# A hybrid convolution and attention block: eight plain products for four query and key jobs, another order for the scaling of x and for the last pair

## Chip, cores and metric

One core of one Trainium2 chip runs the kernel. The metric is the time of one execution on the device in microseconds (us); the number that stands for the kernel is the median of several executions.

## The reference

The block takes x (1 x 2048 x 1024, float32). After an RMS norm with a shift and a scale that come from a small vector c, one projection with 10,240 columns feeds everything else: a causal convolution of 31 taps with two gate inputs, 12 heads of dilated window attention, and the gates that mix the two branches. Cut to what matters here:

```python
mod = jax.nn.silu(c) @ w_ada + b_ada
shift, scale, gate = jnp.split(mod, 3, axis=-1)
h = rms_norm(x, norm_w) * (1.0 + scale) + shift
z = h @ w_in
a, b, g_conv, q, k, v, g_attn, m_conv, m_attn = jnp.split(z, SPLIT_POINTS, axis=-1)
u = depthwise_causal_conv(a * sigmoid(b), conv_w, conv_b)
y_conv = (silu(layer_norm(u, ...)) * silu(g_conv)) @ w_conv_out
q = rope(rms_norm(q, q_norm_w), positions)
k = rope(rms_norm(k, k_norm_w), positions)
outs, lses = dilated_window_attention(q, k, v, window, dilation)   # three groups of four heads
o = sum(softmax(lses) * outs)
y_attn = (o * silu(g_attn)) @ w_attn_out
y = sigmoid(m_conv) * y_conv + sigmoid(m_attn) * y_attn
x = x + gate * (y @ w_out)
```

## The kernel before

**The projection.** The tokens are worked in two halves of 1024. A job is a block of 256 columns for one half. The block is cut in four (token quarters times column halves), and `qkv_quad` (L530) or `quad` (L346) computes it with seven products in place of eight, in the manner of Strassen and Winograd: `PRODUCTS` (L167) pairs A11, A12, A22 and the sums S1 to S4 of quarters of h with B11, B21, B22 and the sums T1 to T4 of quarters of the weights. One product (`product`, L338) is 12 matmuls of 128x512: both factors are split in a high and a low half, and three of the four terms are taken over four pieces of the contraction.

**The weights.** `column_steps` (L260) loads four blocks of weights by SP's queue (names wB11 and so on), makes T1 to T4 on GpSimd (L274), splits each in a high half (ScalarE, L279) and a low half (L280; GpSimd, or VectorE for the products that `QKV_LO` lists), and in the first half also stores each T to DRAM (L285). The second half loads these T's again, seven loads a job rather than four.

**What follows a product.** In `qkv_quad` the results are gathered in two PSUM banks, z and s: four copies on ScalarE (L546) and three additions on VectorE a job. `rotate` (L615) then normalises and rotates q and k: squares on ScalarE, sums over the head by matmuls (pss), rows, a transpose (L655), a root on GpSimd (L664), for k a transpose back and a spreading matmul (L684, L693), 12 VectorE operations for the rotation, and a store to `qk_d`. `turn_v` (L600) transposes v on TensorE.

**The order of the work.** A slot is one product. `slots` lists which job's which product stands in each slot. All other work hangs in an agenda by slot and place (`at_slot`, L506), and the main loop (L1541) writes it out slot by slot; this written order is the order on TensorE, and on VectorE, ScalarE, GpSimd and SP's queue too, but for a stretch in the gates where the scheduler orders the latter four. Weights are asked for five slots ahead and split three slots ahead (`AHEAD`, L39).

The first half begins with plain V jobs of two pairs (slots 0 to 15, `plain_quads`: products without sums). Slots 16 to 127 hold the jobs of `QUADS` (L1081): q and k of pairs 0 and 1, then q, k and v of pairs 2 to 5. From slot 128 come the gates and the convolution's a and b, and the attention of the first half. The second half starts at slot 282 with V, has its first four q and k jobs at some 296 to 325 and its gates from about 408 to 561. The output projections follow.

**Work without a slot of its own.** The convolution's VectorE operations (`conv_parts`, L388) wait in `conv_todo`. After each slot the main loop adds `PACE` (L42) to a credit, takes off what VectorE operations of the slot cost by the kernel's own estimate (`Counted`, L200), and runs pieces while the credit lasts:

```python
credit = min(max(credit, -2.0) + PACE[i >= half_jobs] - spent[0], 2.0)
while conv_todo and credit > 0.35:
    run_conv(1)
```

The second half's x is loaded, squared (`later_x`, `later_square`, L1320) and scaled (`later_scale`, `later_sum`, L1358, L1365; 32 VectorE operations in four groups) while the first half's q, k and v jobs run. The scalings are laid by hand into slots 42 to 67 by a list `room` (L1392). Only then is the SBUF that they use given to the attention (`free_at`, L1454). At the turn of the halves the quarters A12, A22 and S1 to S4 of the second half land from DRAM and are split (`quarter_split`, L182; names landing).

## Time and profile before

| what | value |
|---|---|
| runs, us | 2378.17, 2378.13, 2377.22; median 2378.13 |
| profiled execution, own time | 2384.58 us |
| its span | 2382.7 us |
| its mean granted TensorE clock | 0.989 |
| GpSimd (POOL) busy in the span | 1120.5 us, 47% |
| HBM traffic | 284.98 MB read, 164.24 MB written |

The span goes from the first to the last instruction of the profiled execution; its own time is 1.9 us more, and lies 6.45 us above the median of the runs. In the profile, PE is TensorE, PEld its weight loads, DVE VectorE, ACT ScalarE, POOL GpSimd and SP the engine that issues the DMAs. The page gives busy time by engine and by group; the windows give it for a stretch (busy time, count of instructions, granted clock, share of the DMA engines, GB/s); the waits give what ended an engine's idle time. A recorded matmul's time overlaps the next one's, and a few per cent of the matmuls may be missing from the records.

### The profile page before, as it was taken

To read this page: it belongs to the slowest core of one execution; us is meant where nothing else is said; L and a number is where in the kernel's file an instruction comes from. 1 tells how busy PE (TensorE), PEld (TensorE's weight loads), DVE (VectorE), ACT (ScalarE), POOL (GpSimd) and SP (SyncE) were. 2 spreads that over 40 slices of the span, in tenths; PEclk is the share of its full clock that TensorE was granted. 3 is DMA by queue.
4 is the path that set the end of the run, shared out by engine and by line. 5 is a ranking of instruction groups with operands and counts; after the bars stand their busy time and mean duration, and the time that the engine had idled before them with its cause. 6 is when DMAs were issued, how large, how long until landed. Compare 5 with 4: busy or idle time off the path is not lost. (4 is left out here: it accounts for less than half of the span.)

```text
span 2382.7 us, 34400 instructions
## 1 busy us (share of the span) xinstructions
PE 2293.4 (96%) x11386; PEld 1864.2 (78%) x11386; DVE 1740.3 (73%) x2838; ACT 1113.5 (47%) x2267; POOL 1120.5 (47%) x878
## 2 busy tenths in 40 slices
PE   6899899999999999989999999999999999999999
PEld 4677678887888887867788887877888888888887
DVE  6768874657979789847757557599997957796644
ACT  4754355555654444644455444554444444332221
POOL 2366544455557788936433333445666740000221
PEclk9999999999999999999999999999999999999999
DMA  7656766676654454643665665756444579875553
GB/s 258 193 174 222 234 175 205 194 219 202 197 171 156 159 189 151 203 150 115 181 191 174 208 186 179 232 153 194 137 137 144 168 250 321 290 236 188 182 161 102
DMA packets 304107, 451.54 MB, mean 190 GB/s; under 512 B 29236, under 2 KB 132788, under 8 KB 303928
## 3 DMA queue, kind: packets, MB, share of 16 engines
q1 hardware_dynamic: 289656, 423.62, 56.2%
q10 hardware_dynamic: 14272, 25.72, 2.9%
q8 instruction: 90, 1.47, 0.3%
q14 instruction: 89, 0.73, 0.1%
HBM read 284.98 MB, written 164.24 MB: 189 GB/s over the span
## 5 line engine op out<-in xcount | busy, mean ns | idle before, releaser
L280 POOL TENSOR_TENSOR slT<-wT,shT 128x512 fp32r<-128x512 f32 x188 | 260.6, 1387 | 312.4 <-ACT shT L279 294.9
L280 POOL TENSOR_TENSOR slB<-wB,shB 128x512 fp32r<-128x512 f32 x164 | 219.1, 1337 | 187.8 <-ACT shB L279 176.7
L279 ACT ACTIVATE shB<-wB 128x512 fp32r<-128x512 f32 x234 | 147.7, 631 | 180.5 <-issue 34.8
L280 POOL TENSOR_TENSOR slT<-wB,shT 128x512 fp32r<-128x512 f32 x98 | 132.7, 1357 | 144.7 <-ACT shT L279 110.8
L208 DVE SCALAR_TENSOR_TENSOR ce<-us,pair_taps,ce 128x512 f32<-128x512 f32 x240 | 180.8, 753 | 5.9
L279 ACT ACTIVATE shT<-wT 128x512 fp32r<-128x512 f32 x192 | 120.7, 628 | 129.1 <-POOL slB L280 23.9
L208 DVE SCALAR_TENSOR_TENSOR ce<-ut,chan,ce 128x512 f32<-128x512 f32 x240 | 180.4, 751 | 0.8
L208 DVE SCALAR_TENSOR_TENSOR cq<-ut,chan,cq 128x512 f32<-128x512 f32 x208 | 156.3, 751 | 4.5 <-ACT cq L409 4.3
L208 DVE CUSTOM_DVE_ANT_0 sm<-ps,mask,rqq 128x256 f32<-128x256 f32 (+1 forms) x192 | 78.1, 444 | 95.1 <-PE ps L837 36.0
L274 POOL TENSOR_TENSOR wB<-wB,wB 128x512 f32<-128x512 f32 x80 | 113.2, 1415 | 54.6 <-DVE slB L208 46.0
L279 ACT ACTIVATE shT<-wB 128x512 fp32r<-128x512 f32 x120 | 75.4, 628 | 71.6 <-PE paab L342 32.6
L137 POOL TENSOR_SCALAR stf<-stf 128x4 f32<-128x4 f32 x4 | 1.9, 474 | 180.2 <-DVE stf L1656 143.5
L893 PE MATMUL po<-v,pT 128*128 128x128 f32 x560 | 81.8, 277 | 2.4 <-ACT pT L870 1.4
L1828 ACT ACTIVATE yh<-yq 128x512 fp32r<-128x512 f32 x48 | 27.4, 624 | 119.8 <-POOL yq L1822 46.2
L893 PEld LDWEIGHTS po<-v,pT 128*128 128x128 f32 x560 | 75.6, 192 | 9.2 <-ACT pT L870 1.9
L208 DVE TENSOR_TENSOR slB<-wB,shB 128x512 fp32r<-128x512 f32 x70 | 55.4, 791 | 30.6 <-ACT shB L279 24.4
L856 ACT ACTIVATE sm<-sm,osb 128x256 f32<-128x256 f32 (+1 forms) x128 | 58.7, 463 | 10.6 <-issue 3.5
L274 POOL TENSOR_TENSOR wT<-wB,wB 128x512 f32<-128x512 f32 x40 | 56.2, 1407 | 2.4
L865 PE MATMUL ptp<-ident,sm 128*128 128x128 f32 x332 | 52.4, 274 | 4.4 <-DVE stm L208 3.9
L865 PEld LDWEIGHTS ptp<-ident,sm 128*128 128x128 f32 x332 | 41.1, 140 | 18.9 <-issue 4.6
L1887 DVE TENSOR_TENSOR xt<-xt,oa 128x512 f32<-128x512 f32 x32 | 22.0, 687 | 45.8 <-PE oa L1900 45.8
L274 POOL TENSOR_TENSOR wB<-wB,wT 128x512 f32<-128x512 f32 x40 | 54.6, 1364 | 0.0
(833 smaller groups left out, 7803.8 us busy)
## 6 DMA issues: line engine op xcount, KB each, us to landing
wB<-in_w_in_dram SPq DMA_DIRECT2D x274, 256.0 KB, 4.0
wT<-tT_d SPq DMA_DIRECT2D x152, 256.0 KB, 3.0
tT_d<-wB SPq DMA_DIRECT2D x114, 256.0 KB, 3.7
qk<-qk_d SPq DMA_DIRECT2D x96, 256.0 KB, 4.0
v_d<-vev SPq DMA_DIRECT2D x48, 256.0 KB, 3.5
qk_d<-spare_hi SPq DMA_DIRECT2D x48, 256.0 KB, 4.0
qk_d<-spare_lo SPq DMA_DIRECT2D x48, 256.0 KB, 4.1
v<-v_d SPq DMA_DIRECT2D x96, 128.0 KB, 3.9
```

What stands on the lines that cost most here:

```text
L137: nc.gpsimd.tensor_scalar(scratch, src, EPS, None, op0=ALU.add)
L208: return f(out, *args, **kw)
L274: nc.gpsimd.tensor_tensor(dst, x0, x1, op=ALU.subtract)
L279: nc.scalar.activation(h, q[name], AF.Copy)
L280: eng.tensor_tensor(l, q[name], h.bitcast(F32), op=ALU.subtract)
L856: nc.scalar.activation(sm[:, a:z], sm[:, a:z], AF.Exp, scale=-1.0, bias=box["low"][i], accum_out=box["total"][i])
L865: nc.tensor.transpose(pt[:, c : c + P], box["sm"][:, c : c + P], ident)
L893: nc.tensor.matmul(po[:, P * i : P * i + P], box["pT"][:, c : c + P], vt, start=(m == 0), stop=(m == count[i] - 1))
L1828: nc.scalar.activation(h, src, AF.Copy)
L1887: add = lambda dst, ps: tc.keep_in_program_order(nc.vector.tensor_tensor(dst, dst, ps, op=ALU.add))
```

## The change

- The first half's (Q,0), (K,0), (Q,1), (K,1) become `qkv_plain` jobs: eight plain products each on A11, A21, A12, A22 with the four loaded weight blocks. No T's, no additions; four copies by ScalarE, the banks z and s in turn; all four low halves on GpSimd. The kernel has 566 products in place of 562, and all slots behind these jobs count four more.
- A21 stays in its buffer until then, so S4, which takes that buffer, is parked in DRAM (`s4_d`, stored in slots 15 to 18, loaded again in 44 to 47).
- The second half's jobs of the same columns find no stored T's, so they make them afresh on GpSimd, with four loads, and split the weights of products 1, 3 and 5 on VectorE.
- The second half's x is loaded and squared a slot apart rather than two, and its 32 scalings are taken from the credit like the convolution's pieces (`run_later`). The attention's memory opens at slot 65 (`LATER_END`).
- `PACE` has a value for each of four stages: 2.75, 3.05, 2.5, 2.85 in place of 2.95.
- The last pair runs k, q, v in place of q, k, v; the stores of its results lose their special places, and the convolution's tiles open a slot earlier.

The diff, cut to its core:

```diff
-PACE, AGAIN = (2.95, 2.95), 12
+PACE, AGAIN = (2.75, 3.05, 2.5, 2.85), 12
+PLAIN_QK, LATER_END = 4, 65
 MANUAL, ORDER_END = (True, True), 6
-LATER_X, LATER_ROOM, LATER_BUSY = 21, 2, 1
+LATER_X = 20
...
+    PLAIN_8 = (("B11", "A11", 0), ("B11", "A21", 1), ("B21", "A12", 0), ("B21", "A22", 1),
+               ("B12", "A11", 2), ("B12", "A21", 3), ("B22", "A12", 2), ("B22", "A22", 3))
+
+    def plain_columns(c0, c1):
+        q, got = {}, []
+        last = []
+        where = {"B11": (0, c0), "B21": (1, c0), "B12": (0, c1), "B22": (1, c1)}
+
+        def fetch(n):
+            name = PLAIN_8[n][0]
+            if n % 2 == 0:
+                t = q[name] = wr.tile([P, 4, P], F32, tag="wr", name=f"w{name}_q{c0}")
+                nc.sync.dma_start(t.rearrange("p k c -> p (k c)"), w_in[where[name][1] // P, where[name][0]])
+
+        def step(n):
+            name = PLAIN_8[n][0]
+            if n % 2 == 0:
+                last[:] = (ws.tile([P, 4, P], F32R, tag=f"s{hl}", name=f"s{hl}{name}_q{c0}") for hl in "hl")
+                nc.scalar.activation(last[0], q[name], AF.Copy)
+                nc.gpsimd.tensor_tensor(last[1], q[name], last[0].bitcast(F32), op=ALU.subtract)
+            got.append(tuple(last))
+
+        return got, step, fetch, None
+
+    def qkv_plain(half, which, pair, got):
+        u0 = 2 * pair
+        g = GROUPS[u0 // NH]
+        reg = [scratch_pair() for _ in range(2)]
+        n = f"{'qkv'[which]}{half}_{pair}"
+        cut, place = token_views(g)
+        rotate(half, which, u0, g, reg, n, slots_of[half, which, pair])
+        ps = {}
+        for m, (_, part, c) in enumerate(PLAIN_8):
+            done = c in ps
+            if not done:
+                ps[c] = bank("zs"[c % 2], f"pp{c}{n}")
+            product(part, ps[c], got.pop(0), not done, done)
+            if done:
+                nc.scalar.activation(place(reg[c // 2], c % 2), cut(ps[c]), AF.Copy)
+            yield
...
-        s0 = at[6] + (u0 == 10)
+        s0 = at[6]
...
-        e4, e5, e6 = at[4], at[5], at[6]
+        e4, e6 = at[4], max(at.values())
...
+            if 7 in at:
+                sq = ((at[3], 0, 0, "act2"), (e4, 1, 0, "act2"), (e6, 0, 1, "act2"), (e6 + 1, 1, 1, "act"))
...
-            start = e6 + 1
+            start = e6 + 1 - (u0 == 10 and which == 0)
...
-            at_slot(e6 + 7, store(0), "vec" if u0 == 10 else "store")
-            at_slot(e6 + 7 + (u0 < 10), store(1), "vec" if u0 == 10 else "load")
+            at_slot(e6 + 7, store(0), "store")
+            at_slot(e6 + 8, store(1), "load")
...
-    QUADS = [(Q, 0), (K, 0), (Q, 1), (K, 1), *((w, p) for p in range(2, 6) for w in (Q, K, V))]
+    QUADS = [(Q, 0), (K, 0), (Q, 1), (K, 1), *((w, p) for p in range(2, 5) for w in (Q, K, V)), (K, 5), (Q, 5), (V, 5)]
...
-        chain = [(qkv_quad, half, *q) for q in QUADS]
+        if half == 0:
+            for q in QUADS[:PLAIN_QK]:
+                slots += [(len(jobs), n) for n in range(8)]
+                jobs.append((qkv_plain, half, *q))
+        chain = [(qkv_quad, half, *q) for q in QUADS[PLAIN_QK if half == 0 else 0 :]]
...
-            return column_steps(half, c0, c0 + P, QKV_LO[half][g])
+            return column_steps(half, c0, c0 + P, QKV_LO[half and (g, cb) not in QUADS[:PLAIN_QK]][g])
...
-        at_slot(17 + k // 2, lambda k=k: part_of("S4", k, hf[4 + k, 0], vec), "act2")
+        at_slot(15 + k, lambda k=k: nc.sync.dma_start(s4_d[k], hf[4 + k, 0]), "store")
+
+    last_a21 = slots_of[0, K, 1][5]
+    parked = {}
+
+    def s4_load(k):
+        parked[k] = wide_raw(f"s4_{k}")
+        nc.sync.dma_start(parked[k], s4_d[k])
+
+    for k in range(4):
+        at_slot(last_a21 - 1 + k, lambda k=k: s4_load(k), "load")
+        at_slot(last_a21 + 1 + k, lambda k=k: quarter_split(0, "S4", k, parked.pop(k), vec), "act2")
...
-            at_slot(LATER_X + 2 * j + 1 + c, lambda j=j, c=c: later_square(j, c), "act2")
-    LATER_0 = LATER_X + 18
+            at_slot(LATER_X + j + 1, lambda j=j, c=c: later_square(j, c), "act2")
+    LATER_0 = LATER_X + 10
...
+    later_todo, later_from = [], {0: LATER_0 + 4, 1: LATER_0 + 4}
+    for k in range(2):
+        at_slot(LATER_0 + 1, lambda k=k: later_load(k), "store")
     for k in range(4):
-        at_slot(LATER_0 + 1 if k < 2 else free[k - 2], lambda k=k: later_load(k), "store")
-        room = [r for r in room if r >= max(when, LATER_0 + 4)]
-        work = [lambda k=k, i=i: later_scale(k, i) for i in range(4)]
+        later_todo += [(k, lambda k=k, i=i: later_scale(k, i)) for i in range(4)]
...
-            work.append(lambda k=k, args=args: later_sum(k, *args))
-        for f in work:
-            when = room.pop(0)
-            at_slot(when, f)
-        free.append(when + 3)
-    later_done = when + 3
+            later_todo.append((k, lambda k=k, args=args: later_sum(k, *args)))
+
+    def run_later(s):
+        k, f = later_todo.pop(0)
+        f()
+        if k < 2 and later_todo[0][0] != k:
+            at_slot(s + 3, lambda: later_load(k + 2), "store")
+            later_from[k + 2] = s + 6
...
-    free_at = [later_done, 0]
+    free_at = [LATER_END, 0]
...
-            k6 = slots_of[half, K, pair][6]
+            q6, k6 = (max(slots_of[half, w, pair].values()) for w in (Q, K))
...
-            ready = max(k6 + 11, v6 + 7, free_at[half])
+            ready = max(q6 + 10, k6 + 11, v6 + 7, free_at[half])
...
-        at_slot(q_end + 7, lambda half=half: conv_open(half), "enter")
+        at_slot(q_end + 6, lambda half=half: conv_open(half), "enter")
...
-        credit = min(max(credit, -2.0) + PACE[i >= half_jobs] - spent[0], 2.0)
+        stage = (i >= gates_start[0]) + (i >= half_jobs) + (i >= gates_start[1])
+        credit = min(max(credit, -2.0) + PACE[stage] - spent[0], 2.0)
         spent[0] = 0.0
-        while conv_todo and credit > 0.35:
-            run_conv(1)
+        while credit > 0.35 and (conv_todo or later_todo and s >= later_from.get(later_todo[0][0], s + 1)):
+            if conv_todo:
+                run_conv(1)
+            else:
+                run_later(s)
```

VectorE, around the first q job of the first half (q0_0), before; slT and slB are low halves of weights, S4_lo the low half of a sum, spare_hi the job's result, to which pbq and pcq are added, and tm its rotation:

```order
L208 TENSOR_TENSOR S3_lo_0_816<-hf3_1_184,S3_hi_0_815 128x512
L208 TENSOR_TENSOR S4_lo_0_955<-hf4_0_177,S4_hi_0_954 128x512
L208 TENSOR_TENSOR S4_lo_0_955<-hf5_0_178,S4_hi_0_954 128x512
L208 TENSOR_TENSOR spare_hi_168<-s1q0_0_937,pbq0_0_960 128x128x4
L208 TENSOR_TENSOR S4_lo_0_955<-hf6_0_179,S4_hi_0_954 128x512
L208 TENSOR_TENSOR S4_lo_0_955<-hf7_0_180,S4_hi_0_954 128x512
L208 TENSOR_TENSOR slB22_0_3584_1017<-wB22_0_3584_752,shB22_0_3584_1016 128x512
L244 CAST pick0_1039<-edge_145 32x128 x2
L208 TENSOR_TENSOR spare_hi_168<-spare_hi_168,pcq0_0_1020 128x128x4
L208 TENSOR_TENSOR slB21_0_5120_1077<-wB21_0_5120_903,shB21_0_5120_1076 128x512
L208 TENSOR_TENSOR spare_hi_168<-spare_hi_168,pcq0_0_1020 128x128x4
```

The same place in the changed kernel:

```order
L210 TENSOR_TENSOR S1_lo_0_777<-hf7_1_189,S1_hi_0_776 128x512
L210 TENSOR_TENSOR hf7_0_181<-hf7_0_181,hf3_0_177 128x512
L210 TENSOR_TENSOR S3_lo_0_810<-hf3_1_185,S3_hi_0_809 128x512
L246 CAST pick0_1001<-edge_146 32x128 x2
L210 SCALAR_TENSOR_TENSOR tmq0_0_00_1122<-spare_hi_169,hw_139,cos0_999 128x512
L210 SCALAR_TENSOR_TENSOR tmq0_0_01_1124<-spare_hi_169,hw_139,sin0_1000 128x512
L210 SCALAR_TENSOR_TENSOR spare_hi_169<-spare_hi_169,hw_139,sin0_1000 128x512
L210 SCALAR_TENSOR_TENSOR spare_hi_169<-spare_hi_169,hw_139,cos0_999 128x512
L210 TENSOR_TENSOR spare_hi_169<-spare_hi_169 128x512
```

The additions of pbq and pcq and the low halves of weights no longer stand there, nor S4's splits; behind S3 come the table rows and the rotation at once.

VectorE at the turn of the halves, before; A22_lo is the last of the landing quarters, cq, co, ce, ca and usum are pieces of the convolution, and pcv is V's bank that is added to its result:

```order
L208 SCALAR_TENSOR_TENSOR A22_lo_1_9842<-landingA22_2_9792,mod_139,A22_hi_1_9841 128x512
L208 TENSOR_TENSOR slT1_1_6912_9872<-wB11_1_6912_9628,shT1_1_6912_9871 128x512
L208 SCALAR_TENSOR_TENSOR cq0_7_9429<-ut0_7_9110,chan_133,cq0_7_9429 128x512 x4
L208 SCALAR_TENSOR_TENSOR co0_7_9910<-ut0_7_9110,chan_133,cq0_7_9429 128x512
L208 TENSOR_TENSOR ca0_7_9912<-ce0_7_9431,co0_7_9910 128x511
L208 COPY ca0_7_9912<-ce0_7_9431 128x1
L208 COPY odd_tail_136<-co0_7_9910 128x1
L208 SCALAR_TENSOR_TENSOR ce0_7_9431<-ce0_7_9431,pair_taps_134,co0_7_9910 128x512
L208 SCALAR_TENSOR_TENSOR ce0_7_9431<-us0_7_9702,pair_taps_134,ce0_7_9431 128x512 x3
L208 TENSOR_TENSOR slB22_1_6656_9939<-wB22_1_6656_9596,shB22_1_6656_9938 128x512
L208 SCALAR_TENSOR_TENSOR ce0_7_9431<-us0_7_9702,pair_taps_134,ce0_7_9431 128x512 x2
L208 TENSOR_TENSOR slB22_1_6912_9958<-wB22_1_6912_9634,shB22_1_6912_9957 128x512
```

And in the changed kernel:

```order
L210 SCALAR_TENSOR_TENSOR A22_lo_1_9813<-landingA22_2_9764,mod_140,A22_hi_1_9812 128x512
L210 TENSOR_TENSOR slT1_1_6912_9842<-wB11_1_6912_9601,shT1_1_6912_9841 128x512
L210 SCALAR_TENSOR_TENSOR ce0_7_9243<-us0_7_9371,pair_taps_135,ce0_7_9243 128x512 x5
L210 SCALAR_TENSOR_TENSOR ca0_7_9559<-us0_7_9371,pair_taps_135,ce0_7_9243 128x512
L210 TENSOR_TENSOR usum0_5250<-usum0_5250,ca0_7_9559 128x1024
L210 TENSOR_TENSOR slB22_1_6656_9904<-wB22_1_6656_9570,shB22_1_6656_9903 128x512
L210 TENSOR_TENSOR slB22_1_6912_9921<-wB22_1_6912_9607,shB22_1_6912_9920 128x512
L210 TENSOR_TENSOR spare_hi_169<-spare_hi_169,pcv1_0_9887 128x128x4
L210 TENSOR_TENSOR spare_lo_170<-spare_lo_170,pcv1_1_9907 128x128x4
L210 TENSOR_TENSOR spare_hi_169<-spare_hi_169,pcv1_0_9887 128x128x4
L210 TENSOR_TENSOR spare_lo_170<-spare_lo_170,pcv1_1_9907 128x128x4
```

Seven rows' worth of convolution (five ce, ca, usum) stand between the last landing and V's additions, where before 25 pieces stood among these and behind them.

SP's queue at the second half's last pair, before; qk10 and qk11 are the stores of the last pair, the w names loads of weights:

```order
L269 DMA wT1_1_8192_14266<-tT1_8192_d_4947 128x512
L920 DMA ai_d_97<-asb8_1_2_14231 128x256
L799 DMA qk9_1_4_14314<-qk9_d_72 128x2x256
L800 DMA v9_1_4_14315<-v9_d_84 128x256
L269 DMA wT3_1_8192_14318<-tT3_8192_d_4987 128x512
L828 DMA part9_1_2_14367<-acc1_d_88 128x2x260
L269 DMA wB22_1_8192_14369<-in_w_in_dram 128x512
L703 DMA qk10_d_73<-spare_hi_168 64x1024
L703 DMA qk11_d_74<-spare_hi_168 64x1024
L703 DMA qk10_d_73<-spare_hi_168 64x1024
L703 DMA qk11_d_74<-spare_hi_168 64x1024
```

And in the changed kernel:

```order
L271 DMA wT1_1_8192_14225<-tT1_8192_d_5028 128x512
L965 DMA ai_d_97<-asb8_1_2_14194 128x256
L746 DMA qk10_d_73<-spare_hi_169 64x1024
L746 DMA qk11_d_74<-spare_hi_169 64x1024
L746 DMA qk10_d_73<-spare_hi_169 64x1024
L746 DMA qk11_d_74<-spare_hi_169 64x1024
L844 DMA qk9_1_4_14273<-qk9_d_72 128x2x256
L845 DMA v9_1_4_14274<-v9_d_84 128x256
L271 DMA wT3_1_8192_14277<-tT3_8192_d_5070 128x512
L873 DMA part9_1_2_14316<-acc1_d_88 128x2x260
L271 DMA wB22_1_8192_14318<-in_w_in_dram 128x512
```

The four stores stand ahead of wT3 and wB22 of that job, where they stood behind them.

22 lines of the change are left out of this document (8 added, 14 removed).

## The prediction

> **What bounds the kernel now.** I read the page's first lines, then the windows of all engines over the stretches that the change touches, then the same windows for the projection's matmuls (L342) alone, then the waits of TensorE.
>
> ```profile
> span 2382.7 us, 34400 instructions
> PE 2293.4 (96%) x11386; PEld 1864.2 (78%) x11386; DVE 1740.3 (73%) x2838; ACT 1113.5 (47%) x2267; POOL 1120.5 (47%) x878
> ```
>
> ```profile
> core 0: us, PE busy (x) PEld busy (x) DVE busy (x) ACT busy (x) POOL busy (x), PEclk, DMA share, GB/s
> 93.00:198.00 105.00, 95.01 (x510) 73.81 (x509) 77.09 (x91) 58.25 (x112) 62.36 (x42) 0.97 0.55 175
> 198.00:318.00 120.00, 107.43 (x529) 82.04 (x528) 97.77 (x125) 48.46 (x83) 65.93 (x41) 0.94 0.70 231
> ...
> 512.00:731.00 219.00, 211.43 (x1094) 177.28 (x1093) 165.18 (x398) 127.49 (x324) 128.06 (x120) 1.00 0.61 199
> 731.00:986.00 255.00, 252.96 (x1110) 208.91 (x1109) 224.74 (x297) 125.30 (x216) 216.75 (x169) 0.99 0.51 176
> 986.00:1052.00 66.00, 56.48 (x245) 45.20 (x243) 45.53 (x54) 30.25 (x48) 38.25 (x28) 0.94 0.38 128
> 1052.00:1136.00 84.00, 81.81 (x392) 65.32 (x391) 53.17 (x58) 39.53 (x66) 48.25 (x34) 0.96 0.41 127
> ...
> 1476.00:1490.00 14.00, 9.62 (x54) 8.25 (x52) 6.04 (x20) 4.62 (x15) 2.79 (x4) 0.93 0.77 242
> ...
> 1705.00:1935.00 230.00, 230.00 (x1012) 189.75 (x1011) 189.99 (x270) 111.08 (x192) 145.27 (x113) 1.00 0.52 162
> ```
>
> ```profile
> core 0: us, PE busy (x), PEclk, DMA share, GB/s
> 93.00:198.00 105.00, 88.13 (x350) 0.97 0.55 175
> 198.00:318.00 120.00, 99.85 (x384) 0.94 0.70 231
> 986.00:1052.00 66.00, 53.42 (x217) 0.94 0.38 128
> 1052.00:1136.00 84.00, 78.94 (x323) 0.96 0.41 127
> ...
> 1705.00:1935.00 230.00, 229.41 (x1008) 1.00 0.52 162
> ```
>
> TensorE is busy for 96% of the span, so a saving can only be fewer matmuls, matmuls at a higher clock, or shorter waits of TensorE. In the last row nothing disturbs it: 230/1008 = 0.228 us a matmul, so a product of 12 takes 2.74 us. Against that, 93 to 318 (slots 16 to 76: the first half's early q, k and v jobs) took 225 us for 350 + 384 = 734 matmuls, which would be 167.5 us. The 57.5 us between them are 14.5 of TensorE's other work (95.01 + 107.43 - 88.13 - 99.85), 22.6 idle (225 - 202.4), and 20.5 in which matmuls ran slowly (188.0 - 167.5). The idle time has these causes:
>
> ```profile
> engine line waited for: us in total, times, longest us
> PE pssk L644 <- ACT sqk L625: 4.8, 2, 2.9
> PE pcq L342 <- DVE slT L208: 3.6, 1, 3.6
> PE pcv L342 <- DVE spare_hi L208: 2.9, 1, 2.9
> PE paq L342 <- ACT stk L660: 2.3, 1, 2.3
> PE pwk L684 <- POOL stk L680: 2.1, 1, 2.1
> PE rsk L693 <- DVE rwk L208: 2.0, 2, 1.7
> ```
>
> A wait costs more than its length. Here is TensorE after the 2.3 us one, and the window of the product behind it:
>
> ```profile
> 156.55 0.50 PE L342 MATMUL paq<-S_hi,shT 128*128 128x512 f32 x1 [2.34 <-ACT stk L660]
> ...
> 157.69 0.63 PE L342 MATMUL paq<-S_hi,shT 128*128 128x512 f32 x1
> 158.12 0.63 PE L342 MATMUL paq<-S_lo,shT 128*128 128x512 f32 x1
> ```
>
> ```profile
> 156.40:161.00 4.60, 4.45 (x13) 3.51 (x13) 2.02 (x3) 2.83 (x9) 4.18 (x2) 0.63 0.80 257
> ```
>
> The matmuls then start 0.43 us apart and the granted clock is 0.63: 4.45 us of work where 2.74 is normal, so 1.7 us more. [...]
>
> **The change part by part.** First the eight-product jobs, in place of `qkv_quad` (its first copy is L546). They add 4 products, 4 x 2.74 = 10.9 us at the full rate. Per job they take from VectorE three additions and three low halves, and from GpSimd four weight sums:
>
> ```profile
> L274 POOL TENSOR_TENSOR wB<-wB,wB 128x512 f32<-128x512 f32 x80 | 113.2, 1415 | 54.6 <-DVE slB L208 46.0 <-DMA v_d<-vev 2.9 <-DMA tT_d<-wB 2.7
> L280 POOL TENSOR_TENSOR slB<-wB,shB 128x512 fp32r<-128x512 f32 x164 | 219.1, 1337 | 187.8 <-ACT shB L279 176.7 <-ACT stq L660 5.0 <-DMA wB<-in_w_in_dram 4.0
> L208 DVE TENSOR_TENSOR slB<-wB,shB 128x512 fp32r<-128x512 f32 x70 | 55.4, 791 | 30.6 <-ACT shB L279 24.4 <-DMA xn<-in_x_dram 5.2 <-issue 0.6
> L208 DVE TENSOR_TENSOR spare_hi<-spare_hi,pcq 128x512 f32<-128x512 f32 x16 | 16.1, 1007 | 48.3 <-ACT spare_hi L546 21.7 <-PE pcq L342 20.1 <-ACT stk L676 6.4
> L208 DVE SCALAR_TENSOR_TENSOR xl<-xl,mod,rsx 128x512 f32<-128x512 f32 x16 | 13.7, 875 | 0.0
> ```
>
> VectorE loses 4 x (3 x 1.007 + 3 x 0.791) = 21.6 us and gets 19 of the 32 scalings of the second half's x, 19 x 0.875 = 16.6 us, in the same 32 slots, but from credit, when a slot has room. GpSimd: four low halves in place of four sums and four low halves that it made (four of seven, VectorE three), so 4 x 4 x 1.415 = 22.6 us less over 88 us of products. The plain job's bank is emptied by one copy on ScalarE, so the banks z and s no longer wait for VectorE: the waits of `pcq` for `slT` and of the next bank go. What is left is the chain of the turns (squares, roots, factors), which the change does not shorten.
>
> How fast is such a stretch with light VectorE? The nearest row is 1052 to 1136, the second half's first four q and k jobs: the same turns, VectorE 53.17 of 84 us (63%, against 77.09 of 105 and 97.77 of 120), and 84/323 = 0.260 us a matmul. The first stretch takes 105/350 = 0.300, the second 120/384 = 0.3125. So the 32 plain slots: 384 x 0.260 = 99.8 us. The other 33 slots (396 matmuls) keep quads, additions and the rest of the scalings, but these have been started earlier: I choose 0.280, a bit under the middle of 0.260 and 0.3125, 110.9 us. Sum 210.7 against 225: **-14**. If all went at 0.260: 780 x 0.260 = 202.8, -22. If the second part stayed at 0.3125: 99.8 + 123.8 = 223.6, -1. S4's eight transfers (parked, reloaded) I cost at nothing: they are asked for two slots, 5.5 us, ahead of their split, about what a landing takes below (1479.05 to 1484.2), with no reader but the S4 product some slots on; one late landing would cost up to 5.
>
> The attention starts 10 slots earlier against the chain (LATER_END 65), and overlaps the convolution's slots by 10 fewer. In 512 to 731, 7.6 us were idle (219 - 211.4); a third less of the crowded slots: **-2**, bounds -6 and +4 (the attention's loads then meet the first part's DMA, 0.70 share).
>
> The half turn, 986 to 1052: 217 matmuls would be 49.5 us, and other matmuls took 3.1 (56.48 - 53.42), so 13.4 us are lost, 9.5 of them idle:
>
> ```profile
> PE pcv L342 <- DVE spare_hi L208: 4.4, 1, 4.4
> PE ptv L606 <- ACT vev L608: 3.0, 2, 2.0
> ```
>
> Ahead of that addition VectorE had convolution pieces, which the new paces (3.05 in the gates) have done by then: behind the last landing split 5 `ce`, `ca` and `usum` are left where 25 pieces were. I take **-11**; bounds -13 and 0, the latter if the landing splits themselves are the delay:
>
> ```profile
> 997.28 4.39 DVE L208 TENSOR_TENSOR S_lo<-landingS,S_hi 128x512 fp32r<-128x512 f32 x3 [1.98 <-ACT S_hi L191]
> ```
>
> ```profile
> 995.00:1005.00 10.00, 10.00 (x45) 8.27 (x45) 7.91 (x9) 7.61 (x12) 10.00 (x7) 1.00 0.08 29
> ```
>
> The three took 1.46 us each, against 0.79 for such an operation elsewhere, with GpSimd busy in all of the window. [...]
>
> The second half's first four jobs (1052 to 1136) now make their T's afresh: 16 sums on GpSimd (22.6 us), 12 low halves moved to VectorE (9.5 us, and 12 x 1.337 = 16.0 off GpSimd), and 12 loads fewer. GpSimd's 48.25 becomes 54.9 and VectorE's 53.17 becomes 62.7 of 84 us, so both still fit: **+1** for their collisions, bounds -3 (loads) and +6 (half of what the first stretch lost to the same work, 105 - 350 x 0.260 = 14, less its clock).
>
> The last pair, keys first:
>
> ```profile
> PE ps L837 <- DVE osb L208: 4.4, 1, 4.4
> ...
> ACT spare_hi L357 <- DMA qk_d<-spare_hi: 8.1, 1, 8.1
> ```
>
> ```profile
> 1479.05 3.38 SPq L703 DMA_DIRECT2D qk_d<-spare_hi  x4
> ```
>
> ScalarE waited 8.1 us, to 1484.29, for these four stores to land before it could write that buffer, and TensorE stood 4.4 us behind it with 0.93 clock. With K ahead of Q and the store two weight loads earlier on SP, the buffer is free a job before it is next needed: **-5**, bounds -5.5 and 0. What comes next there is V's landing, in its old place. The paces of the second half (2.5, 2.85) I cost at nothing: 1705 to 1935 has no idle time, and VectorE has 40 us of slack in 230 to hide pieces that come later.
>
> Sum: -14 - 2 - 11 + 1 - 5 = **-31**. Own time of the profiled execution 2384.58 - 31 = 2353.6; it was 6.45 above the median of the runs, so the median is 2353.6 - 6.45 = **2347**.
>
> **The rivals.** (a) The first part's waits come from the chain of the turns: four of the six rows above wait for `sq`, `st` or `rw`, 11.2 us of the 17.7, and these stay. Then only the 10.9 come on top of what the rest gives: +10.9 - 2 - 11 + 1 - 5 = -6, median 2372. Against: the slow clock also follows the waits for VectorE, and 1052 to 1136 has the same chain. Chance 0.13, half of it within 0.2% (4.8 us, about what a measurement of this kernel can tell from no change). (b) The half turn stays late because of its landing splits: -20, median 2358; chance 0.12. (c) Slower: the gates' pace of 3.05 is more VectorE work a slot than TensorE's 2.74 hide. Were the planner's costs true, VectorE would set the end of each of the 154 slots from the gates to the half turn: 0.31 x 154 = 48, sum +17, median 2395. It decides once a slot's real VectorE work is over 2.74. Against: in 731 to 986, 93 slots at pace 2.95, VectorE worked 224.74, 2.42 a slot; 3.05 makes that 2.50. Chance 0.07. (d) Short waits cost only themselves, and the slow matmuls come from something that stays: then half the idle 22.6 goes and the products cost 10.9, 0 in the first part, -9.5 in the half turn, -4.4, +1, -2: -15, median 2363; the row at 156.55 speaks against it: 0.05. [...] That the change doesn't do what it says is excluded by the order of the instructions.
>
> **How the numbers follow.** The forecast has 0.62, with 0.01 left over. Faster: 0.62 + 0.065 + 0.12 + 0.05 = 0.85; same: 0.065 + 0.01, 0.08; slower: 0.07. Its own bounds run from -22 - 6 - 13 - 3 - 5.5 = -50 (2328) to about -6; the range 2330 to 2374 takes in (a), (b) and (d) and leaves (c) out.
>
> **What would show it.** In the changed profile 16 to 80 take some 211 us with no `pcq` or `slT` wait in the plain jobs; the wait of `pcv` for VectorE at the half turn is gone; ScalarE doesn't wait for `qk_d` before the second half's gates; VectorE stays under 2.74 us a slot in the gates. I am wrong if waits for `sq` and `st` in the plain stretch fill the room, if TensorE waits for `ce` in the gates, or if the second half's first jobs lose over 6 us.

## The result, and the profile after

| kernel | median of runs, us | range | profiled execution: own time, span |
|---|---|---|---|
| before | 2377.68 (4 runs) | 2376.56 to 2378.17 | 2384.58, 2382.7 |
| changed | 2363.7 (4 runs) | 2359.88 to 2367.62 | 2367.32, 2365.1 |

The change makes the kernel 14.0 us faster: ratio 0.9942, 95% interval 0.9919 to 0.9965. The forecast was 31 us. In the profiled executions the difference is 17.3 us.

The changed kernel's page begins like this; TensorE's busy time is the same as before (2293.5 against 2293.4 us), though it runs 48 more matmuls:

```profile
span 2365.1 us, 34440 instructions
PE 2293.5 (97%) x11434; PEld 1866.9 (79%) x11434; DVE 1716.0 (73%) x2826; ACT 1106.4 (47%) x2255; POOL 1107.1 (47%) x866
```

The windows of the changed kernel run from the start of one slot to the start of another (slots 16 to 47, 48 to 80, 132 to 191, 192 to 283, 284 to 301, 302 to 328, and 412 to 415, the first four products of the second half's gates):

```profile
core 0: us, PE busy (x) PEld busy (x) DVE busy (x) ACT busy (x) POOL busy (x), PEclk, DMA share, GB/s
91.20:189.70 98.50, 98.29 (x545) 78.11 (x542) 59.02 (x77) 50.83 (x97) 45.45 (x28) 1.00 0.74 244
189.70:319.20 129.50, 117.00 (x610) 91.16 (x607) 93.70 (x131) 58.03 (x117) 64.47 (x42) 0.96 0.57 180
512.10:726.10 214.00, 204.84 (x1037) 171.30 (x1036) 165.33 (x376) 119.24 (x292) 128.09 (x121) 1.00 0.58 192
726.10:976.30 250.20, 250.20 (x1105) 207.18 (x1104) 221.87 (x316) 126.06 (x218) 218.12 (x170) 1.00 0.52 179
976.30:1033.00 56.70, 53.73 (x246) 44.27 (x244) 34.35 (x37) 28.35 (x46) 39.10 (x29) 0.97 0.51 153
1033.00:1119.90 86.90, 81.73 (x394) 64.49 (x393) 66.45 (x74) 40.73 (x67) 53.57 (x36) 0.98 0.29 88
1461.20:1478.40 17.20, 17.20 (x103) 14.98 (x101) 7.56 (x29) 10.64 (x31) 5.00 (x8) 1.00 0.85 283
```

For the first two rows, these are the kernel before's windows split at the same place (slots 16 to 43, and 44 to 76), and the same first four products of its gates (slots 408 to 411):

```profile
93.00:191.80 98.80, 90.67 (x473) 70.73 (x472) 70.92 (x84) 56.02 (x110) 60.60 (x41) 0.97 0.57 182
191.80:317.80 126.00, 111.57 (x567) 84.91 (x565) 103.74 (x132) 50.49 (x85) 67.48 (x43) 0.95 0.68 223
...
1475.70:1499.50 23.80, 19.42 (x105) 16.65 (x104) 9.82 (x35) 10.79 (x30) 5.88 (x8) 0.93 0.85 276
```

The plain stretch has 32 products where 28 stood, at clock 1.00, with 0.2 us of idle time, and takes as long as before: the stalls that went paid for the four products exactly. Behind it lies the surprise, 129.5 us for 33 slots where the forecast had 110.9. The same row in the windows of the projection's matmuls alone, of the changed kernel and then of the kernel before:

```profile
189.70:319.20 129.50, 102.62 (x396) 0.96 0.57 180
```

```profile
191.80:317.80 126.00, 103.06 (x398) 0.95 0.68 223
```

So TensorE's other work there rose from 8.5 us (111.57 - 103.06) to 14.4 us (117.00 - 102.62), since the attention starts earlier. The projection's part did not get faster. These are TensorE's longest waits there in the changed kernel:

```profile
PE rsk L736 <- DVE rwk L210: 3.5, 2, 2.2
PE pwk L727 <- POOL stk L723: 3.2, 1, 3.2
PE pssk L687 <- ACT sqk L668: 2.4, 1, 2.4
PE pcv L344 <- DVE spare_hi L210: 1.5, 1, 1.5
```

Stage by stage between the same products, changed minus before, in us: ahead of the first q job -1.8; slots 16 to 76 (80) +3.2; up to the gates -1.9; attention beside the gates -5.0; the gates behind it -4.0; half turn -9.5; second half's first jobs +2.4; its other jobs +1.9; first four products of its gates -6.6; attention there +3.4; the rest 0.0. Together -17.9 as rounded; the start of the last product moved by 17.8 (1943.7 to 1926.0).

### The profile page after: what moved, and what is told of

Same layout as the page of the kernel before. It is cut to its first block, busy times and chain, and to the rows that moved or that the text cites. A ratio compares the mean times of both kernels' runs of the same rounds, so it can differ in the third digit from the quotient of the medians.

```text
span 2365.1 us, 34440 instructions
## 1 busy us (share of the span) xinstructions
PE 2293.5 (97%) x11434; PEld 1866.9 (79%) x11434; DVE 1716.0 (73%) x2826; ACT 1106.4 (47%) x2255; POOL 1107.1 (47%) x866
## 5 line engine op out<-in xcount | busy, mean ns | idle before, releaser
L282 POOL TENSOR_TENSOR slT<-wT,shT 128x512 fp32r<-128x512 f32 x172 | 234.7, 1365 | 289.5 <-ACT shT L281 274.6
L282 POOL TENSOR_TENSOR slB<-wB,shB 128x512 fp32r<-128x512 f32 x152 | 202.8, 1335 | 160.5 <-ACT shB L281 146.5
L281 ACT ACTIVATE shB<-wB 128x512 fp32r<-128x512 f32 x222 | 139.8, 630 | 175.7 <-issue 34.0
L281 ACT ACTIVATE shT<-wT 128x512 fp32r<-128x512 f32 x176 | 110.4, 627 | 128.3 <-PE paab L344 22.3
L276 POOL TENSOR_TENSOR wB<-wB,wB 128x512 f32<-128x512 f32 x80 | 110.7, 1384 | 47.8 <-DVE slB L210 42.4
L1879 POOL TENSOR_TENSOR ys<-yq 128x512 f32<-128x512 f32 x8 | 11.1, 1393 | 98.8 <-DMA yq<-y_d 98.8
L276 POOL TENSOR_TENSOR wT<-wB,wB 128x512 f32<-128x512 f32 x40 | 54.9, 1374 | 2.3
```

Of the source, the lines that this page charges most:

```text
L276: nc.gpsimd.tensor_tensor(dst, x0, x1, op=ALU.subtract)
L281: nc.scalar.activation(h, q[name], AF.Copy)
L282: eng.tensor_tensor(l, q[name], h.bitcast(F32), op=ALU.subtract)
```

## The experiments

Each run is compared with the kernel before, run beside it on the same chip. That kernel's median was 2380.85 us beside keys_first, no_plain, pace_295 and late_attention; 2382.14 beside fresh_t_alone, late_pace_295, lower_on_vector and six_plain; 2381.49 beside changed_again, plain_store_t, queries_first and six_plain_mended; and 2379.77 beside the three that leave work out. So ratios are compared, not times. A number behind a time is such a ratio, with its 95% interval. Stretches are read from one profiled execution each.

**The changed kernel once more.** No edit.

> The changed kernel itself, beside the other runs of this call on one chip. Both theories: 10 to 16 us under the kernel before, as in its first measurement (14.0).

2368.61 us, 0.9944 (0.9923 to 0.9964). The gain is confirmed. Its profiled execution was a long one (span 2376.1), and its slots 48 to 80 took 132.5 us where the first one's took 129.5: how much one execution may say is shown further below.

**The last pair alone** (cut; the attention's start is also held back until the queries are done).

```diff
-    QUADS = [..., *((w, p) for p in range(2, 6) for w in (Q, K, V))]
+    QUADS = [..., *((w, p) for p in range(2, 5) for w in (Q, K, V)), (K, 5), (Q, 5), (V, 5)]
-        s0 = at[6] + (u0 == 10)
+        s0 = at[6]
...
-            start = e6 + 1
+            start = e6 + 1 - (u0 == 10 and which == 0)
...
-            at_slot(e6 + 7, store(0), "vec" if u0 == 10 else "store")
-            at_slot(e6 + 7 + (u0 < 10), store(1), "vec" if u0 == 10 else "load")
+            at_slot(e6 + 7, store(0), "store")
+            at_slot(e6 + 8, store(1), "load")
```

> The kernel before with the last pair as keys, queries, values alone, with the stores in their common places. Theory (each part acts where its stretch got shorter: the traces show 23.8 us before and 17.2 us after for the first four products of the second half's gates): 5 to 7 us under the kernel before, about 2372 us, and no ScalarE wait for qk_d there. Rival (what the pair gained came from what the other parts moved ahead of it): within 2 us of the kernel before, with the wait still there.

2380.7 us, 0.9997 (0.9985 to 1.0009): no gain. Its windows over slots 325 to 407, 408 to 411 and 412 to 474:

```profile
1128.90:1471.40 342.50, 334.25 (x1918) 277.49 (x1918) 221.17 (x421) 167.27 (x401) 125.87 (x94) 1.00 0.63 188
1471.40:1488.60 17.20, 17.20 (x102) 14.99 (x101) 7.51 (x29) 10.63 (x31) 5.29 (x8) 1.00 0.87 288
1488.60:1698.10 209.50, 201.45 (x948) 166.55 (x947) 178.40 (x340) 100.93 (x222) 106.64 (x90) 0.98 0.56 177
```

The four products got 6.6 us shorter, as the theory has it, but the stretch ahead of them grew by 3.1 (339.4 before) and the one behind by 3.8 (205.7 before). ScalarE's wait for `qk_d` is gone there. The local half of the theory holds; its total fails, and there the rival has the number.

**The last pair undone in the changed kernel.** The same edit the other way round, with the convolution's tiles opened a slot later again.

> The changed kernel with the last pair in the old order (q, k, v, the old places of stores and of the convolution's opening). Theory (keys_first: the 6.6 us won at the start of the second half's gates are given back around it, 3.1 in the jobs ahead and 3.8 in the attention behind): within 2 us of the changed kernel, with 23 to 24 us for those four products. Rival (the forecast's term): 5 us slower.

2372.12 us, 0.9951 (0.9935 to 0.9967) against 0.9944 for the changed kernel beside it. The four products take 24.2 us again and the 83 slots ahead 337.3 rather than 341.3, and ScalarE's wait for `qk_d` is back (7.7 us). Both runs agree that this part is worth little: nothing by the first, 1.7 us by the ratios and 3.5 by the medians of the second, where the intervals overlap.

**Attention opened later, and the pace.** Two edits and both together:

```diff
-PLAIN_QK, LATER_END = 4, 65
+PLAIN_QK, LATER_END = 4, 77
```

```diff
-PACE, AGAIN = (2.75, 3.05, 2.5, 2.85), 12
+PACE, AGAIN = (2.95, 2.95, 2.95, 2.95), 12
```

> The changed kernel with the attention's memory opened at slot 77 rather than 65, where the kernel before had it counted from the gates. Theory (attention work on TensorE left the gates, which got 9 us shorter, for slots 48 to 80, where it takes 6.7 us): the sum of the two stretches changes by 1 to 3 us, so 1 to 3 us slower than the changed kernel. Rival (the early attention is what shortened the gates): 7 to 9 us slower.

> The changed kernel with the old pace, 2.95 in all four stages. Theory (the pace of 3.05 in the gates emptied the half turn of the convolution, which was worth 7 us there): 5 to 8 us slower than the changed kernel, with the wait of pcv for VectorE back. Rival (the early attention frees the slots and the convolution ends early by itself): within 2 us of the changed kernel.

> The changed kernel with the attention's memory at slot 77 and the old pace of 2.95 in all stages: the fourth of the square of late_attention (45.0 us for the doubled V jobs), pace_295 (42.0) and the changed kernel (40.8). Theory (either of the two alone takes most of the convolution out of the half turn): 48 to 50 us for the doubled V jobs, as in the kernel before (49.5), and 3 to 5 us slower than late_attention. Rival (the plain jobs or the keys' place did it): 42 to 45 us, no slower than late_attention.

late_attention 2373.21 us, 0.9965 (0.9950 to 0.9981); pace_295 2369.27, 0.9955 (0.9941 to 0.9969); late_pace_295 2377.22, 0.9973 (0.9961 to 0.9986). The doubled V jobs at the half turn (slots 286 to 299, two V jobs side by side), in windows of late_attention, pace_295 and late_pace_295:

```profile
982.90:1027.90 45.00, 40.42 (x180) 32.52 (x181) 38.02 (x46) 20.07 (x32) 29.12 (x21) 1.00 0.27 87
```

```profile
985.20:1027.20 42.00, 41.40 (x179) 33.79 (x180) 29.13 (x35) 20.80 (x32) 29.38 (x22) 0.96 0.42 133
```

```profile
986.90:1036.60 49.70, 43.61 (x179) 34.77 (x180) 43.01 (x53) 20.12 (x31) 29.96 (x21) 0.93 0.24 75
```

The column of VectorE (the third busy time) tells it: 53 instructions and 43.01 us in that stretch with neither edit of the change, 46 with the pace alone, 35 with the early attention alone. With neither, the stretch takes 49.7 us, as before (49.5); the changed kernel takes 40.8. So the early attention alone is worth 7.7 us there and the pace alone 4.7, but the pace only 1.2 beside the early attention. In all, the pace is worth 3 us by the ratios (0.9955 less 0.9942 to 0.9944), under the 5 to 8 that were expected. The theory of the square holds in the stretch; in all, late_pace_295 is 2 us slower than late_attention rather than 3 to 5, and the intervals overlap.

The attention's early start also has a price, in the very slots of the surprise. Slots 48 to 80 of late_attention and, of these, slots 65 to 80; then slots 65 to 80 of the changed kernel:

```profile
191.80:310.10 118.30, 107.77 (x539) 82.17 (x536) 88.68 (x106) 48.38 (x81) 63.15 (x42) 0.96 0.53 175
254.80:310.10 55.30, 51.86 (x253) 40.11 (x252) 34.88 (x48) 22.94 (x38) 27.69 (x19) 0.97 0.49 164
```

```profile
254.90:319.20 64.30, 59.41 (x324) 47.77 (x323) 39.90 (x72) 32.52 (x74) 28.09 (x19) 1.00 0.57 179
```

With the attention opened at slot 77 the 33 slots take 118.3 us rather than 129.5 (late_pace_295: 122.1). Of these 11.2 us, 9.0 lie in slots 65 to 80. The later stages pay for it: in late_attention slots 81 to 131 take 3.3 us more than in the changed kernel, the attention beside the gates 6.0 and the half turn 3.3. That leaves 1.4 us for the early start in these two executions; by the ratios it is worth about 5 (0.9965 less 0.9942 to 0.9944), where 1 to 3 were expected. The intervals overlap, so the size is uncertain.

**No plain jobs.**

```diff
-PLAIN_QK, LATER_END = 4, 65
+PLAIN_QK, LATER_END = 0, 73
```

and S4 split in slots 17 and 18 as before.

> The changed kernel without the eight-product jobs (seven products, stored T's, S4 split where it was before; attention memory opens at slot 73, because the scalings of x do not fit into the credit earlier). Compared with late_attention, which opens it at the same place of the chain. Theory (the plain jobs cost 10.9 us of products and remove about 11 us of stalls): within 3 us of late_attention. Rival (the prediction's sum: plain jobs with the scalings under them are worth 14 us): 14 us slower than late_attention, since the scalings now stand beside additions.

2372.85 us, 0.9970 (0.9959 to 0.9981), late_attention 0.9965: within the 3 us of the theory. The 61 slots from slot 16 on take 220.5 us in no_plain, and the 65 slots from there on 216.9 in late_attention:

```profile
91.30:311.80 220.50, 198.46 (x1030) 152.74 (x1028) 178.68 (x211) 103.82 (x188) 127.37 (x83) 0.96 0.63 207
```

```profile
93.20:310.10 216.90, 206.16 (x1079) 160.31 (x1077) 147.66 (x182) 99.22 (x177) 108.56 (x69) 0.98 0.62 206
```

In themselves the plain jobs win 3.6 us there, net of their four products; late_pace_295, whose slots hold the same work at another pace, takes 220.6, so even that is not told from nothing. And no_plain is 7 us faster than the kernel before: half of the gain comes without any plain job. What the plain jobs do beside is to leave credit for the scalings: in no_plain the last of them run in slot 72 and seven behind slot 69 (slots 76 and 73 of the changed kernel, which runs its last in slot 64), and until they are placed the attention cannot open.

**T's afresh alone, and T's made by the plain jobs.**

```diff
-        fresh = (c0, "T1") not in t_d
+        fresh = (c0, "T1") not in t_d or (half and c0 in [qkv_column(*w) for w in QUADS[:4]])
-            return column_steps(half, c0, c0 + P, QKV_LO[half][g])
+            return column_steps(half, c0, c0 + P, QKV_LO[half and (g, cb) not in QUADS[:4]][g])
```

```diff
             got.append(tuple(last))
+            if n == 4:
+                weight_sum("T1", q["B11"], q["B12"], q["B11"])
+            if n == 6:
+                q["T2"] = wr.tile([P, 4, P], F32, tag="wr", name=f"wT2_q{c0}")
+                weight_sum("T2", q["T2"], q["B22"], q["B11"])
+            if n == 7:
+                weight_sum("T3", q["B12"], q["B22"], q["B12"])
+                weight_sum("T4", q["B21"], q["B21"], q["T2"])
```

where weight_sum subtracts on GpSimd and stores the T a slot later. Since the second half loads these T's, the low halves of its products 1, 3 and 5 also go back from VectorE to GpSimd.

> The kernel before, with only the T's of the second half's first four q and k jobs made afresh on GpSimd and the low halves of products 1, 3 and 5 on VectorE (the stored T's are left unread). Theory (no_plain, which loads them, passes those jobs in 90.1 us, the kernels that make them in 94.2 to 95.5): that stretch takes 4 to 5 us more, 4 us slower in all. Rival (the two first profiles, 94.2 and 94.2): within 2 us of the kernel before, the difference being what the half turn hands on.

> The changed kernel, whose plain jobs also make T1 to T4 on GpSimd and store them, so that the second half loads them as the kernel before does. Theory (the T's made afresh cost the second half's first jobs 3 us by two waits, and GpSimd is idle for half of the plain stretch): the second half's first four jobs take 90 to 92 us rather than 94.2, the plain stretch grows by less than 2 us, 1 to 3 us faster than the changed kernel. Rival (sums beside VectorE's work slow the turns, as they did in the kernel before): the plain stretch grows by 3 to 6 us and eats the gain.

fresh_t_alone 2384.37 us, 1.0008 (0.9995 to 1.0021); plain_store_t 2373.18, 0.9959 (0.9944 to 0.9974). The second half's first four jobs (29 slots), in fresh_t_alone and in plain_store_t, whose plain stretch stands first:

```profile
1037.50:1134.90 97.40, 88.93 (x434) 70.57 (x433) 69.32 (x75) 45.51 (x76) 58.76 (x39) 0.98 0.35 108
```

```profile
92.60:199.20 106.60, 100.05 (x544) 79.04 (x541) 65.28 (x76) 50.84 (x97) 69.77 (x44) 0.98 0.77 252
1039.90:1127.60 87.70, 86.66 (x434) 69.77 (x433) 55.64 (x59) 43.89 (x74) 50.24 (x35) 1.00 0.43 136
```

Against 94.2 us in the kernel before and in the changed one, that is +3.2 and -6.5. Making the T's afresh, with the low halves moved, so costs 3.2 us locally in the one, a little under the theory's 4 to 5, and 6.5 in the other, more than expected. In all it costs 1.9 us in fresh_t_alone, not told from nothing by the interval and within the rival's 2. The rival holds for plain_store_t, and by more than it had: its plain stretch grows by 8.1 us (98.5 in the changed kernel). ScalarE now waits there for transfers and for a weight sum, as its waits show; the changed kernel has none of these in its plain stretch:

```profile
ACT sqq L682 <- DMA v_d<-vev: 4.4, 1, 4.4
...
ACT shT L281 <- POOL wT L276: 3.1, 1, 3.1
ACT S_hi L193 <- DMA s<-s_d: 3.0, 1, 3.0
```

The 16 stores share SP's queue with the loads of x and of S4. The rival's reason, sums beside VectorE's work, is there too: VectorE is busy for 65.28 us with 76 operations, where the changed kernel's 77 take 59.02. How the 8.1 us divide between the two is not shown.

**One small GpSimd operation moved to VectorE.** In the changed kernel, GpSimd's queue behind the last plain job reads thus:

```profile
197.56 3.37 POOL L707 TENSOR_TENSOR stk<-stk,mhalf 128x16 f32<-128x16 f32 x1
200.90 1.28 POOL L282 TENSOR_TENSOR slB<-wB,shB 128x512 fp32r<-128x512 f32 x1
202.27 1.60 POOL L276 TENSOR_TENSOR wB<-wB,wB 128x512 f32<-128x512 f32 x1
203.95 1.59 POOL L276 TENSOR_TENSOR wT<-wB,wB 128x512 f32<-128x512 f32 x1
205.50 0.67 POOL L723 TENSOR_TENSOR stk<-stk 128x16 fp32r<-128x16 f32 x1
```

The root of the k factors, a low half of weights and two weight sums (L276) stand ahead of the small subtraction that TensorE waits for (`pwk`, 3.2 us).

```diff
-            nc.gpsimd.tensor_tensor(lo, r, hi.bitcast(F32), op=ALU.subtract)
+            (nc.gpsimd if half else vec).tensor_tensor(lo, r, hi.bitcast(F32), op=ALU.subtract)
```

> The changed kernel with one small GpSimd operation of each first-half k job, the low half of its factors (L723, 0.67 us), on VectorE. In the changed kernel it stands behind three sums of weights in GpSimd's queue, and TensorE waits 3.2 us for it at 203 to 206. Theory (the first quads' weight sums and the last plain job's turn collide in GpSimd's queue): that wait falls under 1 us and slots 48 to 80 lose 3 to 5 us, 3 to 4 us faster in all. Rival (the chain of the turn is long in itself, the next link in it is VectorE's): the wait moves to rwk on VectorE and the stretch stays within 1 us.

2375.6 us, 0.9966 (0.9953 to 0.9979), some 5 us slower than the changed kernel. The theory falls, and more is lost than the rival had: slots 48 to 80 take 133.6 us, and the wait has grown:

```profile
PE pwk L727 <- DVE stk L210: 10.7, 2, 6.3
```

VectorE is later than GpSimd there. Which load makes both late was still open, so three kernels leave work out.

**Loads left out.** The scalings of x (the credit still counts them), the weight sums of pairs 2 and 3, and both (the first diff is cut: the sums of x are left out in the same way):

```diff
-        stt(q, q, mod[:, KC + kk : KC + kk + 1], xh["rs"][:, 512 * t : 512 * t + 512], ALU.mult, ALU.mult)
+        spent[0] += 0.12 + 512 / 860
```

```diff
         def combine(name, dst, x0, x1):
+            if half == 0 and c0 in [qkv_column(w, p) for w in (Q, K, V) for p in (2, 3)]:
+                q[name] = q[{"T1": "B11", "T2": "B22", "T3": "B12", "T4": "B21"}[name]]
+                return
```

> The changed kernel without the 32 VectorE operations that scale and sum the second half's x (their loads, stores and places in the credit stay; the second half is computed from unscaled x). The forecast took the 33 slots behind the plain jobs at 0.280 us a matmul, 111 us, and they took 129.5 and 132.5. Theory (GpSimd's queue, with its weight sums and roots, is what is late there): 126 to 133 us. Rival (VectorE's load, the forecast's reason): 115 to 121 us.

> The changed kernel without the weight sums T1 to T4 of pairs 2 and 3 in the first half (24 GpSimd operations, 34 us, half of them in slots 45 to 80; the T's are replaced by the blocks they would be made from, so these columns are computed with wrong weights, in both halves). Theory (GpSimd's queue): slots 48 to 80 take 118 to 124 us, with no wait of pwk for GpSimd at slot 52, 6 to 8 us faster in all at most. Rival (VectorE's load): 127 to 133 us.

> Both left out together: the scalings of the second half's x and the weight sums of pairs 2 and 3 in the first half. Theory (GpSimd's queue): within 2 us of no_sums in slots 48 to 80. Rival (VectorE's load): within 2 us of no_scalings. If neither alone moved the stretch and this one takes it to 118 us or less, both engines share the blame; if it stays over 125 us, the waits belong to the chain of the turn itself.

2367.5 us, 0.9947 (0.9929 to 0.9965); 2355.26, 0.9885 (0.9864 to 0.9906); 2362.29, 0.9907 (0.9876 to 0.9938). Slots 48 to 80 of the three, in this order:

```profile
189.30:314.90 125.60, 115.09 (x609) 89.95 (x606) 83.09 (x119) 58.11 (x117) 64.97 (x42) 0.97 0.59 186
```

```profile
190.00:306.50 116.50, 111.60 (x609) 87.96 (x606) 79.41 (x131) 57.85 (x117) 37.15 (x24) 1.00 0.63 203
```

```profile
190.40:306.60 116.20, 111.73 (x611) 88.06 (x607) 72.94 (x119) 57.93 (x117) 35.22 (x24) 1.00 0.64 203
```

Five executions that keep all of this work and open the attention early took 127.5 to 132.5 us there (changed, changed_again, pace_295, queries_first, plain_store_t). Without the sums the changed kernel's stretch loses 13.0 us (129.5 to 116.5), more than the theory had; without the scalings 3.9, just beyond that spread and the theory's range; and with the sums gone, leaving the scalings out too brings 0.3 more. In all, no_sums gains some 14 us on the changed kernel (0.9885 against 0.9942 to 0.9944), about twice the 6 to 8 that were expected at most; no_scalings gains nothing, and both together no more than the sums alone. Where the sums cost is seen in slots 48 to 64, of the changed kernel and of no_sums:

```profile
189.70:254.90 65.20, 57.59 (x288) 43.38 (x285) 53.80 (x60) 25.51 (x43) 36.38 (x24) 0.92 0.57 181
```

```profile
190.00:244.30 54.30, 52.46 (x288) 40.09 (x284) 44.03 (x60) 25.37 (x43) 21.35 (x13) 1.00 0.65 210
```

10.9 of the 13.0 us lie in these 17 slots. There GpSimd's sums are the cause, as the theory had it, and the scalings cost something only while the sums are there. They are not the only cause in the stretch: late_attention keeps them and is 11.2 us faster, most of it in the 16 slots behind. No kernel leaves out both; 54.3 us and late_attention's 55.3 add up to 109.6, an estimate that is near the forecast's 110.9.

VectorE's busy time falls from 93.70 to 79.41 us without one of its operations gone, since it runs 131 instructions in both: a row of the changed kernel, and the same operation of no_sums with GpSimd's row beside it:

```profile
201.04 1.70 DVE L210 SCALAR_TENSOR_TENSOR tmk<-spare_lo,hw,cos 128x512 f32<-128x512 f32 x1
```

```profile
198.99 0.75 DVE L210 SCALAR_TENSOR_TENSOR tmk<-spare_lo,hw,cos 128x512 f32<-128x512 f32 x1
```

```profile
197.01 2.93 POOL L710 TENSOR_TENSOR stk<-stk,mhalf 128x16 f32<-128x16 f32 x1
```

It takes 1.70 us beside GpSimd's 128x512 operations (200.90 and 202.27 above), and 0.75 beside the root of 128x16. In the whole changed execution, 67 such operations of the rotation ran with no 128x512 TENSOR_TENSOR of GpSimd beside them and took 0.73 to 0.75 us; the 24 that had one beside them for over half of their time took 1.40 on the mean. So a sum on GpSimd is paid three times here: in its own queue (1.60 and 1.59 us for the two above), in VectorE's slower operations (1.40 us on the mean against 0.73 to 0.75), and in the clock that TensorE loses by waiting for either (0.96 against 1.00).

**Six plain jobs.**

```diff
-PLAIN_QK, LATER_END = 4, 65
+PLAIN_QK, LATER_END = 6, 67
-    last_a21 = slots_of[0, K, 1][5]
+    last_a21 = slots_of[0, K, 2][5]
```

and, in the mended one,

```diff
+        if g == 2 and 7 in at:
+            sq = ((e6, 0, 0, "act2"), (e6, 1, 0, "act2"), (e6 + 1, 0, 1, "act"), (e6 + 1, 1, 1, "act2"))
```

> The changed kernel with two more plain jobs, (Q,2) and (K,2): 2 more products (5.5 us), S4 parked until after them, 8 more fresh T's in the second half, the attention's memory at slot 67. Theory (a plain job takes away some 3.5 us of stalls and costs 2.74, and each fresh job costs the second half about 1 us): within 2 us of the changed kernel, 2.74 us a product and no wait in slots 16 to 65. Rival (the waits of slots 49 to 69 belong to the pair's quads, 18.6 us): 5 to 8 us faster.

> The changed kernel with (Q,2) and (K,2) plain as well; in six_plain the squares of these two jobs were taken ahead of their last copy, so that their norms left part of the sum out, here they are taken behind it. Theory (what the first stretch wins, the later stages give back): slots 16 to 82 take 216 to 223 us where the changed kernel takes 228 for 65 slots, and the time is within 3 us of the changed kernel's. Rival (the win stays): 6 to 9 us faster.

six_plain, whose norms of (Q,2) and (K,2) leave out part of their sum, 2369.0 us, 0.9935 (0.9918 to 0.9951), within the theory's 2 us; six_plain_mended 2365.5, 0.9922 (0.9905 to 0.9939). Slots 16 to 82 of the mended one:

```profile
91.80:311.20 219.40, 215.27 (x1175) 170.60 (x1173) 136.24 (x194) 105.75 (x207) 96.96 (x61) 1.00 0.65 207
```

67 products in 219.4 us where the changed kernel takes 228.0 for 65; 8.6 us are won there, and 3.1 in the median against changed_again (2368.61, run beside it). It is just outside the theory's 3 and far from the rival's 6 to 9. The mended kernel has the best time of those that do all the work, and beats the kernel before clearly and the changed one by less than the intervals tell apart.

## Why the prediction was wrong in size

- **The first part (-14; +3.2 measured).** The plain jobs were forecast well: 98.5 us against 99.8. The step that failed is "The other 33 slots (396 matmuls) keep quads, additions and the rest of the scalings, but these have been started earlier: I choose 0.280". They took 129.5/396 = 0.327. That is 18.6 us more than the 110.9, and two loads stood there that the choice did not price; each is measured with the other in place. GpSimd's weight sums, which these slots keep, cost 13.0 us (no_sums), 10.9 of them in slots 48 to 64; the reason behind the choice, VectorE's load of scalings, is worth 3.9 at most (no_scalings). And the attention, opened at slot 65, puts its work into slots 65 to 80: 11.2 us (late_attention), which the forecast counted only where that work left, as the -2 below. With the attention late, the first part takes 216.9 and 220.6 us, 4 to 8 less than the 224.8 before, so even then little more than half of the 14 at most. The yardstick misled me: in the second half's first jobs I read light VectorE from the row. GpSimd is as busy there (48.25 of 84 us, against 65.93 of 120), but the T's are loaded there, not summed, and TensorE has only 2.9 us of other work (81.81 - 78.94). That the kind of GpSimd's work matters more than its amount is argued from these rows; no run tests it alone.
- **Attention beside the gates (-2; -5.0, and in changed_again +2.4).** Inside its bounds. Late_attention is at +1.0 there, so the early start did move work out of this stretch; its cost in slots 65 to 80 was put at nothing.
- **Half turn (-11; -9.5).** Right in size, and the wait of `pcv` is gone (one of 3.0 us of `pav` for ScalarE is left). The cause was half right: the early attention took the convolution out of it more than the pace, so the size is partly luck.
- **The second half's first jobs (+1; +2.4).** Within the bounds. fresh_t_alone and plain_store_t put making the T's afresh at 3.2 and 6.5 locally, the second just over the bound of 6.
- **The last pair (-5; -6.6).** The local reading was right, and ScalarE's wait for `qk_d` is gone. But the term did not reach the end: keys_first gained 0, queries_first lost 1.7 by the ratios. Keys_first gave the gain back in the jobs ahead (+3.1) and in the attention behind (+3.8), both of which I had priced at nothing; what in them got slower is open.
- **Gates (0; -4.0), and the ends of both.** VectorE worked 221.87 us in 250.2, 2.41 a slot over 92 slots (the forecast's 93 were 92 too), so rival (c) was rightly held unlikely. Rival (a), at 2372, had the first part keep its waits; 12.7 of 22.6 us of idle time stayed, and in no_sums 7.6 of them are gone, so they belonged to the sums more than to the turn's chain. Rival (d), at 2363, has nearly the measured number and the right sum for the first part, none, but not by its mechanism: clock was lost there (0.96). None of the signs of being wrong that I had named came: TensorE waits for nothing in the plain stretch, has no idle time in the gates (250.20 of 250.2 us busy), and the second half's first jobs lose 2.4 us. The miss lay in slots 48 to 80, which no sign watched.

## What to carry to other kernels

A stretch that serves as a yardstick must have the same work on every engine, not only on the one that is suspected: list what each engine does in both before taking its rate. Work that is moved earlier must be priced where it lands as well as where it leaves. Leaving out one engine's load at a time is quick, and tells which load costs where the waits name several releasers; reading the result slot by slot shows whether a second cause stands behind the first. And a wait that is removed at one place is worth its length only if an experiment with this part alone moves the end.
